# One level of Strassen's algorithm in the MLP of a hybrid decoder layer

## The chip, the cores and the metric

The kernel runs on one core of a Trainium2 chip. The metric is the device time of one execution in microseconds; the time of a kernel is the median of several runs. The profile is of one execution, and its span reaches from the first to the last instruction. The engines are called PE (matrix products; PEld is its loading of stationary operands), DVE, ACT, POOL and SP (which issues DMAs).

## The reference

One layer of a decoder trunk on 2048 prompt tokens and 64 sample tokens, model width 1024, in float32. A token mixer (dilated attention, an SSD scan, a short convolution, behind one input and one output projection) is followed by the MLP, which is what is changed:

```python
D_MODEL = 1024
D_FF = 4 * D_MODEL
...
        x = x + rms_norm(mix, norm_mix_post[l])
        h = rms_norm(x, norm_mlp_pre[l])
        f = jnp.square(jax.nn.relu(h @ w_mlp_up[l])) @ w_mlp_down[l]
        x = x + rms_norm(f, norm_mlp_post[l])
```

Further outputs are the attention caches shifted by eight tokens (16 copies of 2 MB from DRAM to DRAM) and the new states.

## The kernel before, in words

Every large product of float32 matrices is made of three matrix products of split operands: `A.copy` rounds an operand to its high part (type float32r), and a subtraction gives the low part. `mm3` (line 241) then issues hi x lo, hi x hi and lo x hi into one PSUM bank, the first argument being the stationary operand.

There are three stages. The *front* (`front`, line 1205) is the input projection with convolutions, SSD and prompt attention, in four blocks of 512 tokens. Then comes the *output projection* with the sample's attention, tile by tile of 128 tokens; it writes the rows `x2_d` to DRAM. Then the *MLP*. Work is written by generators: a main one emits a little tensor work per step, side streams are advanced in between (`stream`, `poll`). A stream yields how many microseconds of tensor work, by a formula of the kernel's own (columns / 2400, times 4 for plain float32, transposes columns / 1200), shall pass before its next step. Tile's scheduler then fixes the order of instructions on each engine and in each queue from its own estimate of time, and places the semaphores. All of a tag's tiles share that tag's slots; a new tile waits until a slot's last reader is done.

The MLP before goes over four blocks of tokens (512, 512, 512, 576; `MBlk`, line 1467) and in each over 16 groups of 256 of the 4096 hidden columns. `mlp_up` (line 1557) loads and splits, for 128 hidden columns at a time, the up weights (1024 x 128) and the down weights (128 x 1024), each as two raw tiles of 128 x 512 (`split_w`, line 1509: ACT casts, POOL subtracts); it accumulates over eight contraction chunks, and squares the ReLU. In the last block the columns go as 2 x 288. `mlp_down` (line 1581) runs one group behind: for each tile of 128 tokens and each half of the 1024 output columns it multiplies the group's two hidden chunks and adds the bank to an accumulator in SBUF. `mlp_out` (line 1599) norms a finished tile and adds the residual. Tokens are transposed on the tensor engine (`turn`, line 283). `mlp_ahead` (line 1529) prepares the first tokens and weights of the MLP while the output projection still runs.

## Time and profile before

| | |
|---|---|
| time, median of 3 runs | 2829.78 us (2826.06 to 2832.83) |
| span of the profiled execution | 2816.5 us; the profile gives no other time of that execution |
| PE busy | 2691.1 us, 96% of the span, 14369 matmuls |
| DVE, ACT, POOL busy | 51%, 37%, 45% |
| granted PE clock, mean | 0.983 |
| DMA | 419.16 MB, all of it issued by SP |
| first matmul of the MLP | 1285.3 us |

A row of a group reads: line, engine, operation, output <- inputs, shape, count, then busy time and the mean duration of one in ns, then the engine's idle time just before and what ended it. A row of a timeline begins with its start and its length in us. In the views by window the first two columns are the window and its length, then busy time and count of each engine, the granted PE clock, the share of the DMA engines' time and GB/s. Tile views give minimum, median and maximum duration in ns. Line numbers are those of the kernel before.

### The profile page before, as it was taken

What the parts mean: (1) busy time and instruction counts of PE and PEld (TensorE: products, weight loads), DVE (VectorE), ACT (ScalarE), POOL (GpSimd) and SP (SyncE); (2) the same over time, 40 slices, a digit from 0 to 9 for tenths busy, and PEclk for the clock granted to TensorE, in tenths of its full rate; (3) what the DMA queues carried; (4) which work ended last, traced back from release to release, by engine and by line L of the source; (5) the groups of instructions that cost most, each with busy time, mean ns of one, the idle gap of its engine ahead of it and who ended that gap; (6) DMA issues with size and microseconds to landing.
All of it is one profiled execution on the core that took longest, in us unless ns stands there. A gap on an engine that the chain in (4) does not pass through costs nothing.

```text
span 2816.5 us, 39903 instructions
## 1 busy us (share of the span) xinstructions
PE 2691.1 (96%) x14369; PEld 2218.0 (79%) x14369; DVE 1429.8 (51%) x2675; ACT 1049.0 (37%) x2386; POOL 1262.1 (45%) x1218
## 2 busy tenths in 40 slices
PE   7998999999999879999999999999999999999997
PEld 6997777778878646567888887888878888888886
DVE  4645445456554665554443463444554345554555
ACT  3534335345454223344233343322523334232232
POOL 4545443333554432236444464444654446343443
PEclk9999999999999989999999999999999999999998
DMA  6646975555555286455334454333443445332331
GB/s 189 178 134 210 265 208 163 150 182 180 159 180 148 93 247 202 143 188 184 127 90 130 132 170 126 124 127 120 153 142 120 132 130 166 108 113 69 119 112 42
DMA packets 445744, 419.16 MB, mean 149 GB/s; under 512 B 64427, under 2 KB 370131, under 8 KB 445033
## 3 DMA queue, kind: packets, MB, share of 16 engines
q1 hardware_dynamic: 445544, 416.61, 48.2%
q8 instruction: 113, 1.85, 0.3%
q14 instruction: 87, 0.70, 0.1%
HBM read 347.50 MB, written 102.43 MB: 160 GB/s over the span
## 4 chain that ended last, share of the span: by engine, by line
PE 57%; DMA 12%; issue 10%; POOL 9%; DVE 8%; ACT 3%; SPq 1%; POOLq 0%; ACTq 0%; DVEq 0%
PE pu L111 19%; PE pd L111 19%; PE po L111 6%; PE pj L111 6%; DMA raw<-in_w_mlp_up 3%; DMA wraw<-in_w_in 3%; PE pk L111 3%; POOL d L1523 2%; POOL u L1523 2%; PE pt L115 2%; POOL wlo L363 2%; DMA m<-o_d 1%; DVE xh L578 1%; POOL acc L1613 1%; DVE bc L804 1%
## 5 line engine op out<-in xcount | busy, mean ns | idle before, releaser
L111 PE MATMUL pu<-h2i,u 128*128 128x512 f32 (+1 forms) x2560 | 702.1, 356 | 2.2 <-POOL u L1523 2.2
L111 PE MATMUL pd<-d,fhi 128*128 128x512 f32 (+1 forms) x2176 | 676.8, 392 | 0.1
L1523 POOL TENSOR_TENSOR d<-raw,d 128x512 fp32r<-128x512 f32 x256 | 330.4, 1321 | 576.0 <-ACT d L1522 576.0
L1595 DVE TENSOR_TENSOR acc<-acc,pd 128x512 f32<-128x512 f32 (+1 forms) x510 | 347.1, 684 | 375.9 <-PE pd L111 375.0
L111 PEld LDWEIGHTS pu<-h2i,u 128*128 128x128 f32 x2560 | 455.8, 188 | 76.4 <-POOL u L1523 3.9
L111 PEld LDWEIGHTS pd<-d,fhi 128*128 128x128 f32 (+1 forms) x2176 | 397.8, 185 | 89.3 <-DVE acc L1593 1.4
L111 PE MATMUL pu<-h2l,u 128*128 128x512 f32 (+1 forms) x1280 | 456.8, 357 | 6.9 <-ACT u L1522 3.3
L111 PE MATMUL pd<-d,flo 128*128 128x512 f32 (+1 forms) x1088 | 425.5, 392 | 0.0
L1523 POOL TENSOR_TENSOR u<-raw,u 128x512 fp32r<-128x512 f32 x256 | 333.0, 1313 | 178.6 <-ACT u L1522 177.5
L363 POOL TENSOR_TENSOR wlo<-wraw,whi 128x512 fp32r<-128x512 f32 (+1 forms) x191 | 258.7, 1366 | 306.7 <-ACT whi L362 255.7
L1576 DVE TENSOR_TENSOR rl<-rl 128x512 f32<-128x512 f32 (+1 forms) x160 | 187.2, 1171 | 356.3 <-ACT fhi L1575 355.4
L1522 ACT CAST d<-raw 128x512 fp32r<-128x512 f32 x256 | 141.2, 617 | 562.8 <-issue 331.7
L1522 ACT CAST u<-raw 128x512 fp32r<-128x512 f32 x256 | 158.6, 620 | 344.2 <-DMA raw<-in_w_mlp_up 342.6
L111 PEld LDWEIGHTS pu<-h2l,u 128*128 128x128 f32 x1280 | 241.0, 188 | 46.4 <-ACT u L1522 4.1
L111 PE MATMUL pj<-lo,whi 128*128 128x512 f32 (+1 forms) x720 | 269.6, 374 | 6.1 <-ACT xr L572 4.5
L111 PE MATMUL pj<-hi,wlo 128*128 128x512 f32 (+1 forms) x720 | 259.8, 361 | 0.0
L111 PE MATMUL pj<-hi,whi 128*128 128x512 f32 (+1 forms) x720 | 259.4, 360 | 0.0
L111 PEld LDWEIGHTS pd<-d,flo 128*128 128x128 f32 (+1 forms) x1088 | 201.2, 185 | 47.4
L362 ACT CAST whi<-wraw 128x512 fp32r<-128x512 f32 (+1 forms) x192 | 114.4, 617 | 155.8 <-DMA wraw<-in_w_in 124.4
L111 PEld LDWEIGHTS pj<-lo,whi 128*128 128x128 f32 x720 | 137.3, 191 | 26.6 <-ACT xr L572 6.7
L111 PEld LDWEIGHTS pj<-hi,wlo 128*128 128x128 f32 x720 | 137.3, 191 | 18.3 <-issue 0.7
L111 PEld LDWEIGHTS pj<-hi,whi 128*128 128x128 f32 x720 | 137.5, 191 | 15.4
(298 smaller groups left out, 3986.4 us busy)
## 6 DMA issues: line engine op xcount, KB each, us to landing
raw<-in_w_mlp_up SPq DMA_DIRECT2D x256, 256.0 KB
raw<-in_w_mlp_down SPq DMA_DIRECT2D x256, 256.0 KB
wraw<-in_w_in SPq DMA_DIRECT2D x192, 256.0 KB
out_s_k<-in_cache_attn_k SPq DMA_DIRECT2D x8, 2040.0 KB
out_s_v<-in_cache_attn_v SPq DMA_DIRECT2D x8, 2040.0 KB
xt<-in_x_prompt SPq DMA_DIRECT2D x16, 512.0 KB
xc_d<-th SPq DMA_DIRECT2D x32, 256.0 KB
bc<-acsT_d SPq DMA_DIRECT2D x16, 512.0 KB
```

The lines of the kernel that those rows point to most:

```text
L111: return self.eng.matmul(out, lhsT, rhs, **kw)
L115: return self.eng.transpose(out, in_, identity)
L362: A.copy(hi[:, ks, :], raw)
L363: (V if not loaded and j else G).tensor_sub(lo[:, ks, :], raw, hi[:, ks, :].bitcast(F32))
L578: V.scalar_tensor_tensor(xh[:, :512], xr[:, j:j + 512], cwh(j, c), xh[:, :512], op0=ALU.mult, op1=ALU.add)
L804: V.tensor_scalar(bc[:, h, :], bc[:, h, :], acs[:, i, h:h + 1], 0.0, op0=ALU.subtract, op1=ALU.min)
L1522: A.copy(hi[:, cs], raw)
L1523: G.tensor_sub(lo[:, cs], raw, hi[:, cs].bitcast(F32))
L1576: V.tensor_mul(rl[:, :n], rl[:, :n], rl[:, :n])
L1595: V.tensor_add(B.accs[i][:n, cs], B.accs[i][:n, cs], ps[:n])
L1613: (V if hf and n == TS else G).tensor_add(acc[:n, cs], acc[:n, cs], xr[:n, cs])
```

## The change

The tokens are taken in three blocks of 704 (2 halves of 352, the last with the 64 sample tokens). Both products of the MLP are done as a 2 x 2 block product by Winograd's form of Strassen's algorithm: seven products of half-sized blocks instead of eight, with sums of blocks on both sides. For the up product the tokens are halved into 352 and 352, the contraction into 512 and 512, the hidden columns into 2048 and 2048; for the down product the contraction into 2048 and 2048 and the output into 512 and 512.

* The sums of weight blocks (four for each weight, 4 MB each) are formed in DRAM in the front, in a stream of its own: `weight_sums` copies a quarter of a block on SP's queue, then adds another block to it with an accumulating DMA on POOL's, and so on. The quarters 1, 2 and 3 are read straight from the weights.
* A block is a list of steps: for each of seven up products eight steps, then for each of seven down products eight. In step n the raw weights of step n+4 are loaded (one tile of 128 x 1024, 512 KB) and those of step n+1 split, by ACT and POOL (up) or ACT and DVE (down).
* An up step has two hidden chunks of 128 columns, each four contraction chunks of `mm3` with 352 moving columns; a down step has two contraction chunks for three token tiles (128, 128, 96), with 512 moving columns, and a product stays in its three PSUM banks over all its eight steps.
* Sums on the token side are formed by DVE in place (`up_sums`, `down_split`), sums of results by DVE from PSUM (`up_out`, `down_out`). A product's token operands are split by `s_pair`.
* Cache shifts are issued every 20 steps. Comments and docstrings are removed.

The diff, cut to its core (of the removed functions nothing is shown; they are in the code above):

```diff
+HT = 352
+BT = 2 * HT
+NSP = 12
...
+    wsum = {m: [dpool.tile(shape, F32, name=f"{m}{i}_d") for i in range(1, 5)]
+            for m, shape in (("u", [D // 2, FF // 2]), ("d", [FF // 2, D // 2]))}
...
+    def weight_sums():
+        for m in "ud":
+            n = wsum[m][0].shape[0] // 4
+            (b11, b12), (b21, b22) = corners[m]
+            w1, w2, w3, w4 = wsum[m]
+            for at in range(4):
+                r = slice(n * at, n * at + n)
+                nc.sync.dma_start(w1[r], b11[r])
+                nc.sync.dma_start(w3[r], b12[r])
+                yield 15.0
+                G.dma_start(w1[r], b12[r], accum_op=ALU.add)
+                G.dma_start(w3[r], b22[r], accum_op=ALU.add)
+                yield 20.0
+                nc.sync.dma_start(w2[r], w1[r])
+                yield 15.0
+                G.dma_start(w2[r], b22[r], accum_op=ALU.add)
+                yield 20.0
+                nc.sync.dma_start(w4[r], w2[r])
+                yield 15.0
+                G.dma_start(w4[r], b21[r], accum_op=ALU.add)
+                yield 15.0
+    corners = {}
+    for m, w in (("u", I["w_mlp_up"][0]), ("d", I["w_mlp_down"][0])):
+        r, c = w.shape
+        corners[m] = [[w[i * r // 2:(i + 1) * r // 2, j * c // 2:(j + 1) * c // 2] for j in range(2)]
+                      for i in range(2)]
+    quarters = {m: {1: corners[m][0][0], 2: corners[m][1][0], 3: corners[m][1][1],
+                    5: wsum[m][0], 6: wsum[m][1], 7: wsum[m][2], 4: wsum[m][3]} for m in "ud"}
...
         stream(side())
+        stream(weight_sums(), 40.0)
         yield from in_qkv(b0)
...
+    NJ = FF // P // 2
+    TP = [(0, P), (P, P), (2 * P, HT - 2 * P)]
+    UP_ORDER, DOWN_ORDER = (1, 2, 6, 7, 5, 3, 4), (1, 2, 7, 4, 5, 6, 3)
...
+    steps = [(kind, b, i, jj) for b in range(TT // BT) for kind, order in (("u", UP_ORDER), ("d", DOWN_ORDER))
+             for i in order for jj in range(NJ // 2)]
...
+    def w_load(at):
+        kind, b, i, jj = steps[at]
+        raw = w4.tile([P, 1024], F32, name="wraw4", tag="w")
+        if kind == "u":
+            wload[0] = nc.sync.dma_start(raw.rearrange("p (k c) -> p k c", c=2 * P),
+                                         quarters["u"][i].rearrange("(k p) c -> p k c", p=P)
+                                         [:, :, 2 * P * jj:2 * P * jj + 2 * P])
+        else:
+            wload[0] = nc.sync.dma_start(raw.rearrange("p (j c) -> p j c", c=512),
+                                         quarters["d"][i][2 * P * jj:2 * P * jj + 2 * P, :]
+                                         .rearrange("(j p) c -> p j c", p=P))
+        wts[at] = raw
+    def w_split(at):
+        raw = wts[at]
+        hi = w4.tile([P, 1024], F32R, name="whi4", tag="w")
+        lo = w4.tile([P, 1024], F32R, name="wlo4", tag="w")
+        A.copy(hi, raw)
+        (G if steps[at][0] == "u" else V).tensor_sub(lo, raw, hi.bitcast(F32))
+        wts[at] = hi, lo
+    def s_pair(src):
+        hi = s4.tile([P, HT], F32R, name="shi", tag="s")
+        lo = s4.tile([P, HT], F32R, name="slo", tag="s")
+        A.copy(hi, src)
+        V.tensor_sub(lo, src, hi.bitcast(F32))
+        return hi, lo
...
+            self.q = [], []
...
+                pt = ps.tile([P, 512], F32, name=f"pq{k}", tag=tag)
+                for xt, a, n in self.xs:
+                    PE.transpose(pt[:, a:a + n], xt[:n, k * P:(k + 1) * P], ident[:n, :n])
+                q = (r4 if self.t == 0 else f4).tile([P, HT], F32, name="q", tag="f")
+                A.activation(q, pt[:, :HT], AF.Copy, scale=vec[:, V_MLP + k:V_MLP + k + 1])
+                self.q[k // 4].append(q)
+                yield 1.0
...
+        s4 = p4.enter_context(sb("s4", NSP, "right"))
+        r4 = p4.enter_context(sb("r4", 8, "right"))
+        w4 = p4.enter_context(sb("w4", 8, "right"))
+        h = halves[0, 0] = Half(0, 0, [(w4, "w")])
+        h.rows()
+        yield 12.0
+        yield from h.turn(psS, "s")
+        up_s[0, 1] = [s_pair(q) for q in h.q[0]]
+        for at in range(4):
+            w_load(at)
+        w_split(0)
...
+    f4 = p4.enter_context(sb("f4", 64, "left"))
+    y4 = p4.enter_context(sb("y4", 12, "left"))
+    t4 = p4.enter_context(sb("t4", 2, "left"))
     psD = p4.enter_context(psb("ps4D", 4))
...
+    def bank():
+        nbank[0] += 1
+        ps, tag = ((psS, "s"), (psD, "pd"), (psD, "pd"))[nbank[0] % 3]
+        return ps.tile([P, 512], F32, name="pm", tag=tag)
...
+    def relu2(x, sign):
+        A.activation(x, x, AF.Relu, scale=sign)
+        A.activation(x, x, AF.Square)
+    def up_out(i, j, ps):
+        ps = ps[:, :HT]
+        x = {k[:2]: v for k, v in X.items() if k[2] == j}
+        if i == 1:
+            A.copy(f_tile(1, 2, j), ps)
+        elif i == 2:
+            o = f_tile(1, 1, j)
+            V.tensor_add(o, ps, x[1, 2])
+            relu2(o, 1.0)
+        elif i == 6:
+            V.tensor_add(x[1, 2], ps, x[1, 2])
+        elif i == 7:
+            V.tensor_add(f_tile(2, 1, j), ps, x[1, 2])
+        elif i == 5:
+            o = f_tile(2, 2, j)
+            V.tensor_sub(o, x[2, 1], ps)
+            V.tensor_sub(x[1, 2], x[1, 2], ps)
+            relu2(o, -1.0)
+        elif i == 3:
+            V.tensor_add(x[1, 2], ps, x[1, 2])
+            relu2(x[1, 2], -1.0)
+        else:
+            V.tensor_add(x[2, 1], ps, x[2, 1])
+            relu2(x[2, 1], 1.0)
+    def up_sums(b):
+        (q11, q12), (q21, q22) = halves[b, 0].q, halves[b, 1].q
+        s3 = []
+        for c in range(4):
+            s3.append(f4.tile([P, HT], F32, name="s3", tag="f"))
+            V.tensor_sub(s3[c], q11[c], q21[c])
+            V.tensor_sub(q21[c], q21[c], q22[c])
+            V.tensor_sub(q11[c], q21[c], q11[c])
+            V.scalar_tensor_tensor(q12[c], q12[c], -1.0, q11[c], op0=ALU.mult, op1=ALU.subtract)
+        return {6: q11, 7: s3, 5: q21, 3: q12, 4: q22}
+    def up_split(b, i, cs):
+        up_s.setdefault((b, i), []).extend(s_pair(src[b, i][c]) for c in cs)
...
+    def down_split(b, i, j):
+        x = {k[:2]: v for k, v in X.items() if k[2] == j}
+        if i == 1:
+            a = x[1, 1]
+        elif i == 2:
+            a = x[1, 2]
+        elif i == 7:
+            a = t4.tile([P, HT], F32, name="d3", tag="t")
+            V.tensor_sub(a, x[1, 1], x[2, 1])
+        elif i == 4:
+            a = x[2, 2]
+        elif i == 5:
+            a = x[2, 1]
+            V.tensor_sub(a, a, x[2, 2])
+        elif i == 6:
+            a = x[1, 1]
+            V.tensor_sub(a, x[2, 1], a)
+        else:
+            a = x[1, 2]
+            V.scalar_tensor_tensor(a, a, -1.0, x[1, 1], op0=ALU.mult, op1=ALU.subtract)
+        down_s[b, i, j] = s_pair(a)
+    def down_out(i, p, ps):
+        n = TP[p][1]
+        ps = ps[:n]
+        def y(t, d, new=False):
+            if new:
+                Y[t, d, p] = y4.tile([P, 512], F32, name=f"y{t}{d}", tag="y")
+            return Y[t, d, p][:n]
+        if i == 1:
+            A.copy(y(1, 2, True), ps)
+        elif i == 2:
+            V.tensor_add(y(1, 1, True), ps, y(1, 2))
+        elif i == 7:
+            V.tensor_add(y(2, 2, True), ps, y(1, 2))
+        elif i == 4:
+            V.tensor_add(y(2, 1, True), ps, y(2, 2))
+        elif i == 5:
+            for d in ((2, 2), (1, 2)):
+                V.tensor_sub(y(*d), y(*d), ps)
+        elif i == 6:
+            for d in ((2, 1), (2, 2), (1, 2)):
+                V.tensor_add(y(*d), ps, y(*d))
+        else:
+            V.tensor_add(y(1, 2), ps, y(1, 2))
...
+    for at, (kind, b, i, jj) in enumerate(steps):
+        if at + 4 < len(steps):
+            w_load(at + 4)
+        if at + 1 < len(steps):
+            w_split(at + 1)
+        order = UP_ORDER if kind == "u" else DOWN_ORDER
+        nxt = steps[at + 2] if at + 2 < len(steps) else None
+        if kind == "u" and jj == NJ // 2 - 2 and i != UP_ORDER[-1]:
+            ni = UP_ORDER[UP_ORDER.index(i) + 1]
+            if ni == 6:
+                while b not in done_in:
+                    advance(min(streams, key=lambda st: st[1]))
+                src.update({(b, k): v for k, v in up_sums(b).items()})
+            up_split(b, ni, (0, 1))
+        if kind == "d" and i == DOWN_ORDER[-1] and jj == NJ // 2 - 1 and (b + 1, 1) in src:
+            up_split(b + 1, 1, (0, 1))
+        two = steps[at + 1] if at + 1 < len(steps) else None
+        if kind == "u":
+            hi, lo = wts.pop(at)
+            s = up_s[b, i]
+            for j2 in range(2):
+                ps = bank()
+                for c in range(4):
+                    ws = slice(2 * P * c + P * j2, 2 * P * c + P * j2 + P)
+                    mm3(ps[:, :HT], hi[:, ws], lo[:, ws], *s[c], c == 0, c == 3)
+                up_out(i, 2 * jj + j2, ps)
+        else:
+            hi, lo = wts.pop(at)
+            if jj == 0:
+                banks = [bank() for _ in TP]
+            for j2 in range(2):
+                j = 2 * jj + j2
+                s = down_s.pop((b, i, j))
+                ws = slice(512 * j2, 512 * j2 + 512)
+                for p, (a, n) in enumerate(TP):
+                    mm3(banks[p][:n], s[0][:, a:a + n], s[1][:, a:a + n], hi[:, ws], lo[:, ws], j == 0, j == NJ - 1)
+            if jj == NJ // 2 - 1:
+                for p in range(len(TP)):
+                    down_out(i, p, banks[p])
+        if kind == "u" and jj == NJ // 2 - 1 and i != UP_ORDER[-1]:
+            up_split(b, UP_ORDER[UP_ORDER.index(i) + 1], (2, 3))
+        if kind == "d" and i == DOWN_ORDER[-1] and jj == NJ // 2 - 1 and b + 1 < TT // BT:
+            while (b + 1, 1) not in src:
+                advance(min(streams, key=lambda st: st[1]))
+            have = len(up_s.get((b + 1, 1), []))
+            up_split(b + 1, 1, range(have, 4))
+        if two is not None and two[0] == "d":
+            for j2 in range(2):
+                down_split(two[1], two[2], 2 * two[3] + j2)
+        if kind == "d" and jj == NJ // 2 - 1 and i in (6, 3):
+            for p in range(len(TP)):
+                mlp_out(b, 2 if i == 6 else 1, p)
+        if kind == "d" and i == 6 and jj == 2 and b + 1 < TT // BT:
+            stream(next_block(b + 1))
+        if at % 20 == 10 and shifts:
+            ...
```

More of the change, by code (lines that the diff above doesn't have):

```diff
@@ L1581, in mlp_down @@
-    def mlp_down(B, grp):
-        fs = B.f.pop(grp)
-        if B.accs is None:
-            B.accs = [accp.tile([P, D], F32, name=f"acc{i}", tag="acc") for i in range(len(B.tiles))]
-        for i, (t, n) in enumerate(B.tiles):
-            a = t - B.t0
-            for hf in range(2):
-                cs = slice(512 * hf, 512 * hf + 512)
-                ps = psD.tile([P, 512], F32, name="pd", tag="pd")
-                for c, (fhi, flo, dh, dl) in enumerate(fs):
-                    mm3(ps[:n], fhi[:, a:a + n], flo[:, a:a + n], dh[:, cs], dl[:, cs], c == 0, c == GC - 1)
-                if grp == 0:
-                    V.tensor_copy(B.accs[i][:n, cs], ps[:n])
-                else:
-                    V.tensor_add(B.accs[i][:n, cs], B.accs[i][:n, cs], ps[:n])
-            if grp == NG - 1:
-                mlp_out(B.accs[i], t, n)
@@ L1599, in mlp_out, with f_tile @@
-    def mlp_out(acc, t, n):
+    V.tensor_scalar(g4[:, 512:], g4[:, 512:], -1.0, None, op0=ALU.mult)
+    nbank = [0]
+    def bank():
+        nbank[0] += 1
+        ps, tag = ((psS, "s"), (psD, "pd"), (psD, "pd"))[nbank[0] % 3]
+        return ps.tile([P, 512], F32, name="pm", tag=tag)
+    XT = [(epool, "xres"), (epool, "x2t")]
+    X = {}
+    Y = {}
+    def f_tile(t, f, j):
+        X[t, f, j] = (r4 if (t, f) == (2, 2) and j >= 12 else f4).tile([P, HT], F32, name=f"x{t}{f}", tag="f")
+        return X[t, f, j]
@@ L1602, in mlp_out @@
         for hf in range(2):
[L1603 to L1604 removed]
+            A.activation(jk[:n, 512 * hf:512 * hf + 512], ys[hf][:n], AF.Square, accum_out=ss[:n, hf:hf + 1])
         G.tensor_add(ss[:n, 0:1], ss[:n, 0:1], ss[:n, 1:2])
         r = rstd_of(e4, ss[:, 0:1], n, D)
[L1607 to L1609 removed]
+        pool, tag = XT[xi[0] % 2]
@@ L1610, in mlp_out @@
+        xi[0] += 1
+        xr = pool.tile([P, D], F32, name="x2r", tag=tag)
+        nc.sync.dma_start(xr[:n], x2_d[t0:t0 + n, :])
         for hf in range(2):
             cs = slice(512 * hf, 512 * hf + 512)
-            V.scalar_tensor_tensor(acc[:n, cs], acc[:n, cs], r[:n], g4[:n, cs], op0=ALU.mult, op1=ALU.mult)
-            (V if hf and n == TS else G).tensor_add(acc[:n, cs], acc[:n, cs], xr[:n, cs])
-            nc.sync.dma_start(out[:, cs], acc[:n, cs])
-    B = early["B"]
-    prev = None
@@ new lines, in second_half, with next_block @@
+    def second_half(b):
+        h = halves[b, 1] = Half(b, 1, XT)
+        h.rows()
+        yield 10.0
+        yield from h.turn(psT, "tr")
+        done_in.add(b)
+    def next_block(b):
+        h = halves[b, 0] = Half(b, 0, XT)
+        h.rows()
+        yield 16.0
+        yield from h.turn(psT, "tr")
+        src[b, 1], src[b, 2] = h.q
+        yield from second_half(b)
+    done_in = set()
+    src[0, 2] = halves[0, 0].q[1]
+    stream(second_half(0))
+    for at, (kind, b, i, jj) in enumerate(steps):
[53 more added lines that the diff above has]
+        if at % 20 == 10 and shifts:
+            nm, sr, sb_ = shifts.pop(0)
+            with tc.issue_after(wload[0].ins):
+                nc.sync.dma_start(O[nm][0, sb_, 0:WB - NS].rearrange("t h e -> t (h e)"),
+                                  I[sr][0, sb_, NS:WB].rearrange("t h e -> t (h e)"))
+        poll()
@@ L1638, in hybrid_layer @@
+    drain()
+    assert not shifts
     p4.close()
```

151 lines of the change are left out of this document (31 added, 120 removed).

## The prediction

> **What bounds the kernel now.** I read the page's totals first, then busy time by stage, then the rhythm of single matmuls.
>
> ```profile
> span 2816.5 us, 39903 instructions
> PE 2691.1 (96%) x14369; PEld 2218.0 (79%) x14369; DVE 1429.8 (51%) x2675; ACT 1049.0 (37%) x2386; POOL 1262.1 (45%) x1218
> DMA  6646975555555286455334454333443445332331
> PE 57%; DMA 12%; issue 10%; POOL 9%; DVE 8%; ACT 3%; SPq 1%; POOLq 0%; ACTq 0%; DVEq 0%
> ```
>
> ```profile
> core 0: us, PE busy (x) PEld busy (x) DVE busy (x) ACT busy (x) POOL busy (x), PEclk, DMA share, GB/s
> 0.00:1000.00 1000.00, 916.38 (x5740) 788.41 (x5740) 541.18 (x1328) 444.75 (x1138) 442.27 (x486) 0.97 0.60 176
> 1000.00:1285.00 285.00, 267.25 (x1422) 177.54 (x1421) 156.18 (x401) 101.46 (x292) 77.18 (x109) 0.97 0.58 185
> 1285.00:2802.00 1517.00, 1507.50 (x7208) 1252.06 (x7208) 724.64 (x942) 501.44 (x953) 733.50 (x614) 1.00 0.39 125
> ```
>
> The stage from 1285 us on is the MLP. The tensor engine is busy there 1507.5 of 1517 us at granted clock 1.00, the DMA engines only 0.39 of the time: it is a tensor-engine stage, so fewer matmul columns are worth their full time as long as nothing else takes over. The stage before it, where the weight sums are put, is another matter: 84 of its first 1000 us pass with the tensor engine idle, and DMA is at 0.60, up to 0.9 in a slice of 70 us.
>
> The chain of waits names the same engine with only 57%, but it gives the rest to feeders that the engine never waits for; busy time by stage is the better guide here.
>
> A matmul's recorded duration overlaps its neighbour's, so I take the spacing of starts. These are the first and last rows of undisturbed stretches of the timeline:
>
> ```profile
> 1292.50 0.39 PE L111 MATMUL pu<-h2l,u 128*128 128x512 f32 x1
> ...
> 1302.30 0.39 PE L111 MATMUL pu<-h2l,u 128*128 128x512 f32 x1
> ...
> 2500.13 0.29 PE L111 MATMUL pu<-h2l,u 128*128 128x288 f32 x1
> ...
> 2503.30 0.30 PE L111 MATMUL pu<-h2l,u 128*128 128x288 f32 x1
> ...
> 2509.14 0.39 PE L111 MATMUL pd<-d,flo 128*128 128x512 f32 x1
> ...
> 2512.54 0.39 PE L111 MATMUL pd<-d,flo 128*128 128x512 f32 x1
> ```
>
> One such row comes in every three matmuls. Up, 512 columns: 42 matmuls in 9.80 us, 0.2333 us each. Up, 288 columns: 24 in 3.17 us, 0.132. Down, 512 columns: 15 in 3.40 us, 0.2267. The two up forms lie on a line (0.000452 us a column, 0.002 fixed), so 352 columns cost 0.161.
>
> ```profile
> L111 PE MATMUL pu<-h2i,u 128*128 128x512 f32 x1536 | 492.0, 396 | 2.2 <-POOL u L1523 2.2
> L111 PE MATMUL pu<-h2i,u 128*128 128x288 f32 x1024 | 210.2, 295 | 0.0
> L111 PE MATMUL pd<-d,fhi 128*128 128x512 f32 (+1 forms) x2176 | 676.8, 392 | 0.1
> L111 PEld LDWEIGHTS pu<-h2i,u 128*128 128x128 f32 x2560 | 455.8, 188 | 76.4 <-POOL u L1523 3.9
> L115 PE MATMUL pt<-cst,xt 128*128 128x128 f32 x256 | 45.7, 293 | 14.3 <-DVE xt L280 11.7 <-DVE lo L296 2.7
> ```
>
> **The change part by part: matmuls.** One of mm3's three products has rows of its own (h2l, flo) at half the count of the rows shown, so before there are 2304 up matmuls of 512 columns, 1536 of 288, and 3264 down matmuls: 2304 x 0.2333 + 1536 x 0.132 + 3264 x 0.2267 = 537.5 + 202.8 + 740.0 = 1480.3 us. After, up: 3 blocks x 7 products x 16 column chunks x 4 contraction chunks x 3 = 4032 of 352 columns, 4032 x 0.161 = 649. Down: 3 x 7 x 16 contraction chunks x 3 token tiles x 3 = 3024 of 512, 685.5. Together 1334.5: **-146 us**. Down gains less than an eighth (7.4%) because 352 tokens cut into 128, 128 and 96, and the 96 pay as much as 128. Transposes, 45.7/256 = 0.18 us each: 136 become 144, +1.4; in the MLP stage 104 become 120. The weight loads (188 ns recorded) don't set the rhythm: 288 columns already come every 132 ns.
>
> The rows before the MLP's end also give what it loses now: 1514.6 us from the first up matmul (1285.3) to the last down one (2799.9, below), less 1480.3, less 104 x 0.18 = 15.6 us.
>
> The Trainium skill ("TensorE: Matmul & The Clock Gate", section Back-to-back issue gap) gives a warm gap of N/2.4 + 2.5 ns; the rows here are longer (233 ns where it has 216). By its figures the saving would be an estimated 135 us, so the sum by it ends 11 us higher; I go by the rows.
>
> **Feeding an up step.** A step is 24 matmuls, 24 x 0.161 = 3.86 us. In it one 1024-wide raw tile is cast by ACT and subtracted by POOL. The output projection's weights show both at that width:
>
> ```profile
> L1069 ACT CAST wohi<-woraw x8: 1028/1042/1052, 931.6 to 968.3; 128x1024 fp32r<-128x1024 f32 x8
> L1070 DVE TENSOR_TENSOR wolo<-woraw,wohi x4: 1225/1432/2804, 933.3 to 965.4; 128x1024 fp32r<-128x1024 f32 x4
> L1070 POOL TENSOR_TENSOR wolo<-woraw,wohi x4: 2350/2384/2627, 934.5 to 969.4; 128x1024 fp32r<-128x1024 f32 x4
> ```
>
> The pool w4 has 8 slots: at any time four raw tiles, and hi and lo of the running step and of the next. So hi of step n+1 goes where hi of step n-1 was, and its cast can start when step n-1's last matmul ends. Then 1.04 + 2.4 + about 0.15 for two handovers = 3.6 us. It is first wanted 3.86 us (hi) and 3.86 + 0.32 (lo, the third matmul) later. Slack about 0.55 us, thin. ACT is in order: in steps of products 2, 5, 3 and 4 it also has two squared ReLUs of two operations each.
>
> ```profile
> L1574 ACT ACTIVATE rl<-pu 128x288 f32<-128x288 f32 x64 | 26.0, 408 | 33.3 <-PE pu L111 31.3 <-DVE flo L1577 2.1
> L1575 ACT ACTIVATE fhi<-rl 128x288 fp32r<-128x288 f32 x64 | 28.4, 445 | 1.9
> L1595 DVE TENSOR_TENSOR acc<-acc,pd 128x512 f32<-128x512 f32 x480 | 326.9, 685 | 349.2 <-PE pd L111 348.4
> ```
>
> At 352 columns about 0.47 each, so ACT has 1.04 + 4 x 0.47 = 2.9 of 3.86 us. The cast is free to start as the step turns, the last output's ReLU only about 0.6 us later (a PSUM add first), so I take the cast as first in line: nothing on the path, but 0.1 us a step for slips, 168 x 0.1 = 17 us. If the order were the other, see the second rival.
>
> DVE's own subtractions share SBUF with POOL. The same 288-wide form beside a POOL subtraction, and alone:
>
> ```profile
> 2498.78 2.76 POOL L1523 TENSOR_TENSOR d<-raw,d 128x512 fp32r<-128x512 f32 x2
> 2498.84 1.53 DVE L1576 TENSOR_TENSOR rl<-rl 128x288 f32<-128x288 f32 x1 [1.95 <-ACT fhi L1575]
> ...
> 2505.21 0.46 DVE L1576 TENSOR_TENSOR rl<-rl 128x288 f32<-128x288 f32 x1
> ```
>
> POOL subtracts 2.4 of each 3.86 us in up steps, so such an operation of 352 columns lies between 0.55 and 0.55 x 1.53/0.46 = 1.8 us, near 1.2 in the mean. On the path these are: the second half of the operand pairs at 18 changes of product, which may only start in the last step (0.5 us each, 9 us); and up_sums, sixteen such operations, ten of them with the first pairs ahead of the next product, 12 us against the 7.7 us of the two steps in which they are emitted: 5 us a block, 15 us. Additions that read PSUM keep 0.68 us whatever POOL does.
>
> The Trainium skill ("SBUF — State Buffer", section Terms) calls the DVE and POOL port pair an exclusive lock, held for the full instruction. By that a subtraction beside a 1024-wide one would wait up to its whole length, not half of a pair as above; by an estimate these two terms would then grow from 24 to about 40 us. This is the page that speaks most against the change, and the rows bear it out in kind.
>
> **Feeding a down step.** 18 x 0.2267 = 4.08 us. ACT 1.04 + 2 x 0.47; DVE one 1.23 us subtraction and two to four of 0.55, POOL idle: hidden. Where a product ends it isn't: product 6 brings 9 additions of 0.685 = 6.2 us to DVE, ahead of the next weights' low part (1.23) and the pairs; about 3 us late, product 5 (6 of them) 1 us, the rest 0.5: 13 us over three blocks. Changes of block, 1.5 us x 3 = 4. All stalls: 17 + 9 + 15 + 13 + 4 = 58 us where there are 15.6 now: **+42**.
>
> **Weight loads.** 512 loads of 256 KB (134 MB) become 336 of 512 KB (176 MB), 131-136 GB/s at full pace beside 125 now at a share of 0.39; rows of the up tiles grow from 512 to 1024 bytes. Issued four steps ahead, some 12 us. The 16 cache shifts stay, a load queued behind one on SP waits for it:
>
> ```profile
> 1320.00:1330.00 10.00, 10.00 (x45) 7.94 (x44) 3.52 (x6) 2.69 (x5) 5.04 (x4) 1.00 0.97 326
> 1340.00:1350.00 10.00, 10.00 (x45) 8.11 (x44) 3.48 (x6) 3.85 (x8) 6.08 (x5) 1.00 0.28 81
> ```
>
> One shift (2.09 MB) fills the DMA engines for under 10 us, less than the lead. Price nothing, covered by that lead; without it, some 3 us x 16.
>
> **The weight sums in the front.** 32 copies of 1 MB on SP's queue and 32 accumulating ones on POOL's, 67 MB of payload. Their emission is paced by estimated matmul time: 40 + 8 x 100, against about 890 of the whole front (my addition of its matmuls with the kernel's own formula), so all goes in ahead of the output projection. The shift above is the nearest row for a copy: 2.09 MB for (0.97 - 0.28) x 10 = 6.9 us of all engines, so 33.5 MB take 110 us. An accumulating one is not in the trace; it reads its target too, so between one and four copies' time, 110 to 440 us. The front has 1000 x 0.40 = 400 us free: sum 220 to 550. So from both sides: hidden (0; a gain is excluded, since nothing leaves the front), or 150 us over. I take it near the lower end, twice a copy, 330 of 400, since it is spread evenly. It still delays others:
>
> ```profile
> ACT whi L362 <- DMA wraw<-in_w_in: 124.4, 71, 6.2
> SPq L358 <- POOL wlo L363: 135.1, 89, 6.7
> PE pk L111 <- DVE dtall L516: 16.6, 5, 6.8
> ```
>
> The input weights arrive just in time: ACT waits for them 71 times. Behind a pair of copies on SP a load is up to 7 us later; POOL's queue holds the wlo subtractions behind each accumulating issue, and that waits for its copy; SP in turn stands at the copy into the next sum until the accumulation has landed. There are 24 such bursts. With three weight pieces in hand (each 24 x 0.2333 = 5.6 us of matmuls) most is absorbed; I put 1 us a burst on the path: **+25** (0 to 90).
>
> **Start and end.** The MLP's first tokens and weights are prepared within the output projection as now, from rows of the first three tiles: no change. The tail:
>
> ```profile
> 2799.54 0.40 PE L111 MATMUL pd<-d,flo 128*64 128x512 f32 x1
> ...
> 2812.67 1.15 SPq L1614 DMA_DIRECT2D out_y_sample<-acc  x2
> ```
>
> 13 us from the last matmul to the last store. After, three token tiles end together instead of one: **+3**.
>
> **Sum.** -146 + 1.4 + 42 + 25 + 3 = -74. The span of 2816.5 becomes 2742. The runs' median of 2829.8 is 13.3 us above the span, and what lies around it stays: 2756.
>
> **The rivals.** *All hidden.* Stalls as now (15.6) and a free front: -146 + 1.4 + 3 = -142, 2688. For it: an engine that is 99% fed now, and DMA at 0.39 in the MLP. Against it: 0.55 us of slack.
>
> *The weight split becomes the bound of the up steps (the other side).* If ACT does the last output's ReLUs (0.6 + 2 x 0.47 = 1.5 us) before the cast, lo is ready 1.5 + 0.1 + 3.5 = 5.1 us after the turn, 0.9 after the third matmul wants it. In all 168 steps +151 - 17: 2756 + 134 = 2890. In the 96 steps with ReLUs alone +69: 2825. It decides from (74 + 17)/168 = 0.54 us a step. For it: a chain of 3.6 in 3.86 us, through two in-order engines. Against it: the cast is ready first.
>
> *The front becomes a DMA stage.* Accumulation at three to four copies' time: 605 + 110 + 385 = 1100 us of DMA in 1000, +85 once pauses count, in place of 25: 2816. For it: the slice at 0.9 and the waits above; against it: the even spread.
>
> *The change doesn't do what it says:* 352-column matmuls paced by the weight load, 188 ns: +110, 2866. Excluded, nearly, by the 132 ns rhythm.
>
> **How the numbers follow.** My forecast 0.50 (by itself 2720 to 2800); all hidden 0.17; split-bound 0.16, of which 0.05 only in part and still faster or level; front 0.13, mostly still faster by half a percent; weight load 0.02; 0.02 beyond. Faster by over 0.2% (5.7 us, about what a measurement of this kernel tells from nothing): 0.50 + 0.17 + 0.03 + 0.09 = 0.79. Within: 0.04. Slower: 0.17. Range 2690 to 2845: it leaves out the full split-bound case and the lowest corner.
>
> **What would show it.** Right: rows of 352 columns every 0.161 us; the MLP's tensor engine above 95% busy; POOL's 1024-wide subtraction near 2.4 us ending before the third matmul of its step; idle gaps of 1 to 5 us at ends of products; the front 20 to 30 us longer. Wrong: PE waiting on lo of the weights in most up steps; DVE subtractions at 2.5 us and more; SP or POOL standing for accumulating DMAs, with the out projection starting 80 us late.

## The result, and the profile after

The changed kernel is slower: 3001.9 us (median, 2998.6 to 3005.4) beside 2829.2 us (2826.1 to 2832.8) for the kernel before in the same session, a ratio of 1.061 (95% interval 1.060 to 1.063). The prediction was 2756 us, range 2690 to 2845: a gain was forecast and a loss came, outside the range.

From the page of the changed kernel: its span, its busy totals (engine, busy us, share of the span, instructions), and three rows of its 40 slices of 75 us each.

```profile
span 2996.8 us, 40429 instructions
PE 2583.9 (86%) x14329; PEld 2189.5 (73%) x14329; DVE 1537.5 (51%) x3001; ACT 1317.8 (44%) x2741; POOL 1049.4 (35%) x908
PE   3013698998999999799999999988999999999997
PEclk7556899999999999899999999999999999999999
DMA  9999746875565654565544444455444446454443
```

The tensor engine is busy 107 us less than before (2583.9 for 2691.1), and the span is 180 us longer. The slices say where: the first five have PE at 0 to 6 tenths, and DMA at 9 in the first four.

Next, busy time by stage of the changed kernel (columns as in the prediction's second fence), first by its three stages (front, output projection, MLP), then the front again in three parts:

```profile
0.00:1205.00 1205.00, 899.37 (x5599) 778.39 (x5600) 512.99 (x1264) 430.26 (x1094) 451.99 (x495) 0.88 0.72 196
1205.00:1533.00 328.00, 297.78 (x1568) 199.45 (x1567) 173.69 (x439) 112.48 (x315) 92.48 (x129) 0.97 0.58 183
1533.00:2984.00 1451.00, 1386.75 (x7165) 1211.70 (x7164) 842.50 (x1292) 774.22 (x1332) 497.18 (x276) 0.99 0.48 159
...
0.00:200.00 200.00, 43.21 (x230) 36.75 (x230) 21.99 (x48) 23.82 (x47) 40.62 (x52) 0.64 1.01 261
200.00:400.00 200.00, 101.44 (x671) 95.83 (x672) 56.92 (x145) 50.78 (x130) 54.30 (x68) 0.73 0.85 211
400.00:1205.00 805.00, 754.72 (x4700) 645.81 (x4700) 434.07 (x1072) 355.65 (x917) 357.07 (x376) 0.97 0.61 176
```

I mark the stages by one group of matmuls, the output projection's (first and last start, from the view of the tile `wohi`; the row of before, then that of after):

```profile
L111 PE MATMUL po<-wohi,clo x272: 387/399/775, 956.9 to 1282.6; 128*128 128x512 f32 x128, 128*64 128x512 f32 x8
```

```profile
L115 PE MATMUL po<-wohi,clo x272: 386/398/629, 1207.0 to 1532.6; 128*128 128x512 f32 x128, 128*64 128x512 f32 x8
```

| | before | after | difference | predicted |
|---|---|---|---|---|
| front, to the first of these | 956.9 | 1207.0 | +250 | +25 |
| output projection | 325.7 | 325.6 | 0 | 0 |
| MLP, from the last of these to the last matmul (2799.5; 2981.4) | 1516.9 | 1448.8 | -68 | about -103 |
| from there to the span's end | 17.0 | 15.4 | -2 | +3 |

The front is the case. All the sums' DMAs run in its first 320 us, although they are emitted over nearly the whole of it. (In this part line numbers are those of the run's own kernel.) The view of the copies of L1220 and of the last accumulations L1232 (forms of the instruction; min, median and max of its ns; first and last start in us):

```profile
L1220 SPq DMA_DIRECT2D u_d<-in_w_mlp_up x4: 573/604/3691, 15.4 to 23.6; - x4
L1220 SPq DMA_DIRECT2D d_d<-in_w_mlp_down x4: 652/2484/33656, 26.4 to 127.2; - x4
...
L1232 POOL DMA_DIRECT2D d_d<-in_w_mlp_down x4: 1012/1012/1014, 275.4 to 304.9; - x4
```

A copy from weights in DRAM into DRAM depends on nothing, so the scheduler, which orders each engine's instructions itself, sets it as early as the queue lets it. The generator's pauses bind the order of emission only. SP then stands at one issue for up to 33.7 us, with the input weights' loads behind it. POOL stands 170 us in all, waiting before its 32 accumulations until earlier DMAs have landed, with its low-part subtractions behind it. The waits in the first 400 us (us in total, times, longest) are those of late loads and of what follows from them:

```profile
ACT whi L369 <- DMA wraw<-in_w_in: 134.3, 25, 38.6
PE pv L119 <- DMA pr<-in_state_ssm_conv: 70.2, 1, 70.2
PE pk L115 <- DVE dtall L523: 64.7, 2, 46.1
PE pk L115 <- POOL wlo L370: 60.6, 4, 29.9
```

Before, ACT waited 6.2 us at the longest for such a weight tile; now 38.6. The granted clock is down to 0.64 and 0.73 in these stretches, so the matmuls that do run cost more as well.

The MLP, waits of the tensor engine from 1533 us on:

```profile
PE pm L115 <- DVE wlo L1528: 24.5, 9, 6.4
PE pm L115 <- POOL wlo L1528: 15.3, 13, 2.5
PE pm L115 <- DVE slo L1536: 11.0, 5, 4.7
PE pq L119 <- DVE xt L287: 6.1, 3, 3.9
PE pm L115 <- ACT whi L1527: 3.6, 6, 0.9
PE pm L115 <- DVE x2t L1157: 1.3, 1, 1.3
```

Together 61.8 us. I went through all starts of the MLP: those that come over a tenth later than usual (0.161 us at 352 columns, 0.232 at 512) are late by 90 us in sum. So 28 more pass in matmuls that follow each other slowly, with hardly a wait; 14 of them lie in the eight stretches of 3.4 or 6.8 us in which the granted clock was 0.50. The timeline behind the wait for `xt` shows a part of these:

```profile
1604.95 0.58 PE L119 MATMUL pq<-cst,xt 96*128 96x96 f32 x2 [3.89 <-DVE xt L287]
...
1606.27 0.50 PE L115 MATMUL pm<-shi,wlo 128*128 128x352 f32 x1
1606.56 0.49 PE L115 MATMUL pm<-slo,whi 128*128 128x352 f32 x1
...
1608.49 0.32 PE L115 MATMUL pm<-shi,whi 128*128 128x352 f32 x1
1608.65 0.32 PE L115 MATMUL pm<-shi,wlo 128*128 128x352 f32 x1
```

and by windows around it:

```profile
1604.00:1609.00 5.00, 4.04 (x18) 4.05 (x19) 5.00 (x11) 2.76 (x7) 0.35 (x1) 0.66 0.35 105
1609.00:1614.00 5.00, 4.97 (x31) 4.68 (x31) 4.59 (x11) 4.30 (x9) 3.01 (x1) 1.00 0.00 2
```

After 3.89 us of idling, 352 columns come every 0.29 us for about 3 us, then every 0.16; the granted clock of these 5 us is 0.66, then 1.00. The Trainium skill ("TensorE: Matmul & The Clock Gate", section What's actually happening) puts the engine at half its clock after an idle window of some 3.4 us, until it has been busy for as long; 352 columns at the half clock that it states would be an estimated 0.293 us, and the trace agrees.

### The profile page after: what moved, and what is told of

Its sections match the earlier page's. It is cut to its first block, busy times and chain, and to the rows that moved or that the text cites. A ratio compares the mean times of both kernels' runs of the same rounds, so it can differ in the third digit from the quotient of the medians.

```text
span 2996.8 us, 40429 instructions
## 1 busy us (share of the span) xinstructions
PE 2583.9 (86%) x14329; PEld 2189.5 (73%) x14329; DVE 1537.5 (51%) x3001; ACT 1317.8 (44%) x2741; POOL 1049.4 (35%) x908
## 3 DMA queue, kind: packets, MB, share of 16 engines
q0 software_dynamic: 10752, 33.56, 6.0%
## 4 chain that ended last, share of the span: by engine, by line
PE 46%; DVE 7%; DMA 4%; POOL 3%; ACT 2%; issue 2%; SPq 0%; POOLq 0%; ACTq 0%; DVEq 0%
PE pm L115 39%; PE po L115 4%; DMA m<-o_d 1%; DVE wlo L1528 1%; POOL wlo L1528 1%; DMA xt<-x_d 1%; DVE slo L1536 1%; POOL rstd L259 1%; POOL rstd_ms L258 0%; PE psq L115 0%; DMA kn<-in_cache_attn_k 0%; PE pt L119 0%; DVE x L1679 0%; ACT whi L1527 0%; PE pos L115 0%
## 5 line engine op out<-in xcount | busy, mean ns | idle before, releaser
L1527 ACT CAST whi<-wraw 128x1024 fp32r<-128x1024 f32 x336 | 351.9, 1047 | 349.3 <-PE pm L115 305.0
L1528 POOL TENSOR_TENSOR wlo<-wraw,whi 128x1024 fp32r<-128x1024 f32 x168 | 410.2, 2442 | 270.9 <-ACT whi L1527 239.7
L115 PE MATMUL pm<-slo,whi 128*128 128x352 f32 x1344 | 439.3, 327 | 14.3 <-DVE slo L1536 9.4
L115 PE MATMUL pm<-shi,whi 128*128 128x352 f32 x1344 | 437.3, 326 | 0.0
L115 PE MATMUL pm<-shi,wlo 128*128 128x352 f32 x1344 | 412.9, 328 | 15.4 <-POOL wlo L1528 15.3
L115 PE MATMUL pm<-wlo,shi 128*128 128x512 f32 (+1 forms) x1008 | 401.2, 398 | 24.6 <-DVE wlo L1528 24.5
L115 PE MATMUL pm<-whi,shi 128*128 128x512 f32 (+1 forms) x1008 | 399.9, 397 | 0.0
L115 PE MATMUL pm<-whi,slo 128*128 128x512 f32 (+1 forms) x1008 | 389.8, 397 | 1.7 <-DVE slo L1536 1.7
L115 PEld LDWEIGHTS pm<-slo,whi 128*128 128x128 f32 x1344 | 256.4, 191 | 17.1 <-DVE slo L1536 9.9
L115 PEld LDWEIGHTS pm<-shi,whi 128*128 128x128 f32 x1344 | 255.9, 190 | 0.1
```

Of the source, the lines that this page charges most:

```text
L115: return self.eng.matmul(out, lhsT, rhs, **kw)
L1527: A.copy(hi, raw)
L1528: (G if steps[at][0] == "u" else V).tensor_sub(lo, raw, hi.bitcast(F32))
```

## The experiments

Theory after the result: (a) the sums' DMAs, drawn forward and in volume, cost the front some 250 us; (b) Strassen's products themselves are worth their predicted gain in the MLP, less stalls at the changes of product. Rivals: the front's loss has another source in the change; the pace is innocent and the volume alone does it, or the reverse; the stalls come from DVE's many operations, as the prediction had it.

**No sums.** The stream of sums is left out, and the four sum quarters are replaced by plain blocks of the same shape.

```
-        stream(weight_sums(), 40.0)
-                    5: wsum[m][0], 6: wsum[m][1], 7: wsum[m][2], 4: wsum[m][3]} for m in "ud"}
+                    5: corners[m][0][1], 6: corners[m][0][0], 7: corners[m][1][0], 4: corners[m][1][1]} for m in "ud"}
```

> The changed kernel without the weight sums: no summing DMA is issued, and the four products that need sums read plain blocks of the weights instead, so the loads keep their number and size but the result of the MLP is another. Theory (the sums, drawn together into the first 305 us, cost the front 250 us): the output projection's first matmul falls from 1205 back to about 955 us, and the time from 3002 to about 2750. Rival (the new MLP is what is slow): the time stays near 3000.

Measured 2767.2 us, ratio 0.978 (0.977 to 0.980). The first output projection matmul (here and below that of the group `po<-wohi,chi`: 955.1 us before, 1205.4 changed) is back at 965.1 us. So the sums cost 235 us (3001.9 - 2767.2). Without them the kernel is 59 us faster than the kernel before in the same session (2826.6), and stands 36 us above the forecast without its term for the sums (2756 - 25 = 2731).

**The sums alone**, added to the kernel before (nothing reads them).

```
 (before)  stream(side())
+        stream(weight_sums(), 40.0)
```

> The kernel before with the weight-sum stream alone added, in the same place and without any tie; nothing reads the sums. Theory: the front is 250 us longer, time about 3080, and the summing DMAs stand at 15 to 305 us as in the changed kernel. Rival (the sums hurt only together with the new MLP's loads): 2830 to 2870.

Measured 3068.6 us (two runs), ratio 1.085 (1.083 to 1.087): 242 us more than before in the same session, the output projection starting at 1198.7 us. The sums' DMAs are issued between 14 and 300 us, as in the changed kernel. The loss in the front needs nothing else of the change.

**Paced.** Each copy is tied behind the last input weight load emitted before it on SP, each accumulation behind the last low-part subtraction of POOL.

```
-                nc.sync.dma_start(w1[r], b11[r])
+                with tc.issue_after(last["sp"].ins):
+                    nc.sync.dma_start(w1[r], b11[r])
...
-                G.dma_start(w1[r], b12[r], accum_op=ALU.add)
+                with tc.issue_after(last["pool"].ins):
+                    G.dma_start(w1[r], b12[r], accum_op=ALU.add)
```

> The changed kernel, but each copy of the sums is tied behind the last input-weight load that was emitted before it on SP, each accumulation behind the last weight subtraction on POOL, so the 64 transfers go in all along the front in place of its first 305 us. Same transfers, same bytes. Theory (their place is what costs): front 955 to 1010 us, time 2755 to 2810, faster than the kernel before. Rival (67 MB more are too much for the front, wherever they are put): front still above 1100, time 2950 or more.

Measured 2882.6 us, ratio 1.019 (1.017 to 1.021): 119 us of the 235 go, 115 stay. The first 200 us now look like this (by windows):

```profile
0.00:200.00 200.00, 171.26 (x1178) 159.48 (x1179) 93.00 (x223) 84.55 (x205) 85.29 (x100) 0.94 0.70 194
```

PE 171 us for 43, DMA 0.70 for 1.01. But the output projection starts at 1087.2 us, 122 later than without sums. Theory and rival are half right each, and the time lies between their ranges: the crowding at the front's start and the volume cost about the same. Whether the crowding costs by full DMA engines or by SP and POOL standing, no run separates.

**Paced, low parts of the down weights on POOL** (which has little to do in down steps; a try at relieving DVE).

```
-        (G if steps[at][0] == "u" else V).tensor_sub(lo, raw, hi.bitcast(F32))
+        G.tensor_sub(lo, raw, hi.bitcast(F32))
```

> As the paced kernel, and the down weights' low part is subtracted by POOL in place of DVE. Theory (the stalls of 4 to 6.6 us behind product 6 of each block, and smaller ones, come from DVE, which has nine additions of PSUM and then the subtraction): these stalls go, 15 to 30 us less than the paced kernel. Rival (POOL's 2.44 us and its hold on SBUF make new waits in 4.08 us steps, DVE's own subtractions first): the same or slower by up to 40 us.

Measured 2942.4 us, ratio 1.040 (1.038 to 1.042), 60 us more than paced: the rival's way, and beyond its 40 us. The tensor engine's longest group of waits in the MLP:

```profile
PE pm L115 <- POOL wlo L1539: 81.8, 28, 9.7
```

Where paced, the waits for both engines' `wlo` summed to 36.7 us. POOL takes 2.4 us for what DVE does in 1.2, and it also holds `mlp_out`'s residual additions in front of it. That pointed to these additions; it doesn't show them to be the cause.

**The residual additions on DVE**, on the kernel without sums.

```
-            (V if hf and b == TT // BT - 1 else G).tensor_add(o[:n], o[:n], xr[:n, cs])
+            V.tensor_add(o[:n], o[:n], xr[:n, cs])
```

> The kernel without weight sums (2767 us; MLP output differs: four sums replaced by plain blocks), with the last residual additions (y plus x2r) all on DVE instead of POOL. Theory: the 6.5 us stall behind product 6 and those of 4 us behind product 3 come from DVE's 1024-wide subtraction (1.21 us alone, 6.47 beside four POOL additions) losing SBUF to POOL. Then that subtraction takes about 1.2 us everywhere in down steps, the stalls shrink to 3 us or less, and the time is 2740 to 2757. Rival (the nine PSUM additions and DVE's queue are the cause, as the prediction had it): DVE gets six more operations at that place, the stall stays or grows, 2767 to 2785.

Measured 2738.9 us, ratio 0.969 (0.967 to 0.972), 28 us less than with the additions on POOL (25 by the ratios), 1 us below the theory's range. In the profiled executions 23 of the 28 lie in the MLP (1456.9 to 1433.9 us). In the kernel without sums, behind product 6 (from the timelines of DVE, POOL and PE):

```profile
1748.10 1.21 DVE L1527 TENSOR_TENSOR wlo<-wraw,whi 128x1024 fp32r<-128x1024 f32 x1
...
1753.71 6.47 DVE L1527 TENSOR_TENSOR wlo<-wraw,whi 128x1024 fp32r<-128x1024 f32 x1
...
1754.17 4.92 POOL L1731 TENSOR_TENSOR y<-y,x2r 128x512 f32<-128x512 f32 x4
...
1760.23 0.79 PE L115 MATMUL pm<-wlo,shi 128*128 128x512 f32 x1 [6.41 <-DVE wlo L1527]
```

and at the same place with the additions on DVE:

```profile
1752.11 1.22 DVE L1527 TENSOR_TENSOR wlo<-wraw,whi 128x1024 fp32r<-128x1024 f32 x1
...
1753.38 0.50 PE L115 MATMUL pm<-wlo,shi 128*128 128x512 f32 x1 [1.27 <-DVE wlo L1527]
```

One subtraction took 6.47 us beside four back-to-back additions of POOL, and takes 1.22 without them. DVE got six operations more there, and the tensor engine's wait of 6.41 us shrank to 1.27 us; the rival falls. POOL's additions end at 1759.09, and 1.21 us later DVE's would end if it had waited for all four: 1760.30, where it ended at 1760.18. The Trainium skill ("SBUF — State Buffer", section Terms) says that the loser of the shared port pair fully blocks; this row agrees, and DVE was kept out over four instructions of POOL.

**Token tiles written out one a step, operand sums three steps sooner**, on top of that.

```
-                mlp_out(b, 2 if i == 6 else 1, p)
+            later = [(b, 2 if i == 6 else 1, p) for p in range(len(TP))]
+        elif later:
+            mlp_out(*later.pop(0))
...
+        if kind == "u" and i == 2 and jj == NJ // 2 - 5:
+            ... src.update({(b, k): v for k, v in up_sums(b).items()})
```

> The same, and two moves in emission: the finished token tiles are written out one a step instead of three at the product's end, and the operand sums of an up phase are made three steps sooner. Theory (stalls are late work of DVE at the change of a product): the 4.8 us wait behind the operand sums goes in two blocks, and the waits behind products 6 and 3 are below 1.5 us; 10 to 20 us below the run with the additions on DVE alone, 2725 to 2742. Rival (the operand sums share SBUF with POOL's weight subtractions wherever they stand, and only move their delay): within 5 us of that run.

Measured 2738.4 us, ratio 0.968 (0.965 to 0.971): no difference that can be measured. The waits of the tensor engine for `slo` in the MLP, of the run with the additions on DVE and of this one:

```profile
PE pm L115 <- DVE slo L1535: 11.1, 5, 4.7
```

```profile
PE pm L115 <- DVE slo L1535: 1.7, 3, 0.6
```

The waits of 4.7 us behind the operand sums did go, and the profiled MLP is 6.9 us shorter, but the front of that execution ran 4 us longer. By its number the rival holds, by its mechanism the theory; it stays undecided.

**Accumulating DMAs as plain copies**, on the paced kernel: the four `accum_op=ALU.add` are left out.

> The paced kernel (2883 us) with its 32 accumulating DMAs as plain copies on the same queue (the sums are wrong by that, the MLP output differs): same bytes written, no read of the target. Theory (the front's remaining 115 us is DMA time): the accumulating DMAs took 180 us of 16 engines and as copies take about 110, so 40 to 70 us come off: 2813 to 2843. Rival (order of issue and the chains between copies cost it, not time in the engines): within 15 us of 2883.

Measured 2823.1 us, ratio 0.999 (0.998 to 1.000), 60 us less (56 by the ratios), within the theory's range. POOL's queue in the paced kernel and here (packets, MB, share of 16 engines' span):

```profile
q0 software_dynamic: 10752, 33.56, 6.4%
```

```profile
q0 software_dynamic: 6656, 33.56, 3.4%
```

6.4% of 2879.8 is 184 us, 3.4% of 2824.1 is 96 us: accumulating costs 1.9 times a copy. 88 us less of DMA time made the kernel 60 us faster, 0.7 of it, where the sums as a whole cost 0.4 of theirs (115 of the 287 us below); why the accumulations weigh more is open. The copies on the other queues cost 103 us more in the paced kernel than in the one without sums (54.5% of 2879.8 less 53.0% of 2766.5), by these rows of the two pages:

```profile
q1 hardware_dynamic: 413896, 492.10, 54.5%
```

```profile
q1 hardware_dynamic: 408008, 458.54, 53.0%
```

Together the sums take 287 us of DMA time, where the prediction put 330.

**Placed.** Additions on DVE and the two moves, full sums. The sums run over four row pieces in turn, so that a dependent DMA is four places behind; those for the up weights go in the front, tied as in the paced kernel; those for the down weights go one every two steps into block 0's up phase.

```
+    def weight_sums(m):
+        for dst, src, add in ((w3, b12, b22), (w1, b11, b12), (w2, w1, b22), (w4, w2, b21)):
+            for at in range(4): ... nc.sync.dma_start(dst[r], src[r]); yield 24.0
+            for at in range(4): ... G.dma_start(dst[r], add[r], accum_op=ALU.add); yield 24.0
...
+        if at % 2 == 0:
+            last["sp"] = wload[0]
+            next(dsums, None)
```

> The whole change with full sums, placed otherwise: additions on DVE and the two moves as in the last run; the sums for the up weights paced over the front, each DMA tied behind the last weight load (SP) or low-part subtraction (POOL) emitted before it, four row pieces in turn so that a dependent DMA is four places behind; the sums for the down weights one DMA every two steps of block 0's up phase, where DMA was 0.4 to 0.56 busy. Theory: the cost of the sums is DMA time in excess of what a stage has free; half of the front's 115 us or less remains (20 to 57), the down sums cost 0 to 20 in the MLP: 2765 to 2815, below the kernel before. Rival: the down sums delay the MLP's weight loads, which are issued 12 us ahead, by bursts of 1 MB (up to 25 us landing): 32 delays of 2 to 5 us, 2830 to 2900.

Measured 2804.0 us, ratio 0.992 (0.989 to 0.994): 0.8% faster than before, clear of noise, and within the theory's range. The output projection starts at 1022.3 us, 56 later than the same kernel without sums (966.0); the MLP takes 1437 us for 1427. Some weight loads in the MLP were held up: with the DMA share at 1.00 from 1420 to 1520 us, the waits for the cast of the weights (`whi`) are 12.8 us in place of 7.0, the longest 6.4. That is far from 32 delays of 2 to 5 us, so the rival falls.

**The front's DMAs made small.** As placed, but each of the up sums' 32 DMAs carries a sixteenth of its rows, and the up products read plain blocks.

```
+                r = slice(n * at, n * at + (n if m == "d" else n // 16))
```

> As the placed kernel (2804 us, first output projection matmul at 1022 us), but each of the 32 DMAs of the up sums carries a sixteenth of its rows, and the up products read plain blocks (so the MLP's output differs). Places, ties, queues and chains of the DMAs stay. Theory (the front pays for DMA time): the output projection starts at 962 to 975 us, the time is 2742 to 2757. Rival (the front pays for the instructions in SP's and POOL's queues and for what stands behind their waits, whatever they carry): the start stays at 1005 us or later, the time above 2785.

Measured 2750.1 us, ratio 0.970 (0.966 to 0.975). The output projection starts at 963.1 us: with the places, ties, queues and chains as they were, the cost is gone. Once paced, the front pays for what the DMAs carry and not for the issues. Shorter DMAs also end waits in the queues sooner, but there was little to end: in the placed kernel POOL waited 0.8 us in all for a copy of the up sums.

**The up sums in the output projection**, one DMA every 8 us of matmuls, tied behind the token tiles' DMAs and additions.

```
-        stream(weight_sums("u"), 40.0)
 (output projection)
+        gap[0] = 8.0
+        stream(weight_sums("u"))
```

> As the placed kernel (2804 us), with the sums for the up weights moved out of the front into the output projection, one DMA about every 8 us of matmuls, tied behind the token tiles' loads, stores and additions. Theory: a sum costs where weight loads arrive just in time (front: 145 us of DMA time cost 58 us there) and little where only the DMA engines' total counts; the output projection has 0.44 of 327 us free, 145 us. So the front returns to about 962 us, the output projection grows by 5 to 30 us: 2750 to 2780. Rival (145 us of sums cost the same 58 us wherever weights or tokens are read meanwhile): 2795 to 2815.

Measured 2797.8 us, ratio 0.989 (0.987 to 0.991). The front is back at 964.5 us as the theory had it, but the output projection takes 367.5 us for 329.8. A window and a group of waits of it:

```profile
1000.00:1100.00 100.00, 70.08 (x307) 45.46 (x308) 45.67 (x128) 23.88 (x71) 28.20 (x40) 0.78 0.94 291
```

```profile
PE pkk L119 <- DMA kn<-in_cache_attn_k: 32.6, 4, 14.6
```

DMA is at 0.94 there, and the sample's cached keys come late. The MLP takes 12 us more than in the placed kernel as well; 9 of them are waits for its token rows (`xt`, 11.1 us for 1.9), 7.2 us in one of them right at its start. The total is the rival's, the split is neither's. Half of the sums, some 144 us of DMA time, cost 56 us in the front (0.39 of itself), 38 in the output projection (0.26) and 10 in block 0's up phase (0.07), where weights are issued four steps ahead; in two other runs with the down sums there the MLP is 9 (half and half) and 16 us (small DMAs) longer than the 1427.

**Half and half**: two of the four up sums in the front from 400 us of matmuls on, the others in the output projection.

```
+        usums.append(weight_sums("u"))
+        stream(itertools.islice(usums[0], 16), 400.0)
```

> As the placed kernel, with the first two of the four up sums in the front, from 400 us of matmuls on (DMA share 0.5 to 0.6 there), and the other two in the output projection at one DMA per 16 us. Theory (cost grows faster than the DMA share): the halves cost 10 to 25 us in the front and 0 to 10 in the output projection: 2752 to 2780. Rival (cost in proportion to the sums' DMA time, 0.4 of it in the front): front 29 and output projection 0, or 29 too: 2775 to 2804.

Measured 2785.2 us (2776.4 to 2793.0), ratio 0.983 (0.981 to 0.986). The front takes 32 us more, the output projection 15, each above the theory's share. The total is in the rival's range, and the front's part (0.44 of 72 us of DMA time) fits its proportional cost; it is still the fastest complete version, 1.7% below the kernel before and 217 us below the changed one.

## Why the prediction was wrong, by its own steps

The steps from the changed kernel to the best one without sums add up, in medians of runs. They come from several sessions, in which the kernel before differs by up to 5 us (2826.2 to 2831.1).

| step | us | change |
|---|---|---|
| the changed kernel | 3001.9 | |
| sums tied to their places | 2882.6 | -119 |
| accumulating DMAs as copies | 2823.1 | -60 |
| no sums | 2767.2 | -56 |
| residual additions on DVE | 2738.9 | -28 |

**The front: the step that failed.** The prediction took the emission to be "paced by estimated matmul time" and "spread evenly", and from that chose twice a copy's time, "330 of 400" us free, and 1 us a burst: +25, in a range of 0 to 90. Two things in it were false.
- Emission order was read as execution order. The sums ran between 15 and 320 us, and that cost 119 us over the same DMAs tied to their places. The prediction's own sign for it, "SP or POOL standing for accumulating DMAs, with the out projection starting 80 us late", came true in kind, with POOL standing 170 us before them and the output projection 250 us late; but the rival had the cause in the accumulation's price, and "against it: the even spread" kept it at 0.13. The upper bound of 150 us was the DMA time in excess of the whole front's; it wasn't the case of all of it coming at once, and the result of 250 lay above it.
- Free DMA time was taken as nearly free of cost. Evenly spread, the sums still cost 115 us for 287 us of DMA time. The prediction had them hidden as long as they fit into the free time, but for 1 us a burst. The small-DMA run shows that what is paid for is what the DMAs carry, not the bursts' instructions.

**The price of the volume: right.** Twice a copy was 1.9 times; 110 us for 33.5 MB of copies was 96 to 103.

**Matmuls, -146: close, about -137.** 352 columns come every 0.161 us, as taken. A down matmul of 512 columns was taken at 0.2267 us; in the changed kernel 45 of them take 10.46 us, 0.232 each:

```profile
1776.52 0.39 PE L115 MATMUL pm<-wlo,shi 128*128 128x512 f32 x1
...
1786.98 0.39 PE L115 MATMUL pm<-wlo,shi 128*128 128x512 f32 x1
```

Over 3024 matmuls that is 16 us more than put. By the mean spacing without the late starts, the MLP's matmuls take 1487 us before and 1350 after. Why 512 columns take 0.232 us here and 0.227 (median of the down matmuls) before is open. The transposes cost less than the 0.18 us put for each: 120 of them some 10 us, not 22. The two errors nearly cancel, so the MLP's total doesn't show them. (The 131 GB/s of a down step is 128, 512 KB in 4.08 us; nothing hangs on it.)

**The stalls of the MLP, 58 us: mis-sized, 90 measured.** The chain of cast and subtraction is no bound: in 168 steps of up, waits for POOL's `wlo` and for `whi` sum to 18.9 us, where 17 were put; the rival of 2890 us didn't occur. DVE's own subtractions, 24 put, cost 11.0 us of waits for `slo`; the operand sums' 5 us a block were 4.7 in two of the three blocks. Token rows cost 7.4 us, where 4 were put for changes of block. The ends of products cost 24.5 us of waits for DVE's `wlo`, where 13 were put. The term of product 6, "9 additions of 0.685 = 6.2 us to DVE", "about 3 us late", was 6.4 in two blocks, and its mechanism was another: POOL's residual additions holding up DVE's subtraction. In the prediction POOL counted as idle in down steps; `mlp_out` was not in that count. Moving them gave 28 us. And no term stood for the other 28 us, of which 14 passed at the lowered clock.

With -137 for the matmuls and stalls of 90 us in place of some 17, the MLP comes out some 66 us shorter; measured are 68.

**Start and end, +3:** -2, nothing.

With the front at its own +25, the changed kernel would have come out at 2767 + 25 = 2792 us: faster than before and inside the range, but 36 us above the forecast, by the MLP's part, which gained 68 us and not 103.

## What to carry to other kernels

A transfer that depends on nothing goes where the scheduler puts it, not where a generator emits it: before pricing background DMAs as spread out, find what ties each to its place, or give it a tie. Even spread out, DMA time in a stage with DMA engines partly free is not free; here it cost 0.3 to 0.4 of itself in the front, whose weights arrive just in time, 0.2 to 0.3 in the output projection, and 0.06 to 0.11 in the MLP's first up phase, whose loads run four steps ahead. That the lead makes the difference is argued, not shown: no run varied it. So an algorithm that saves a tenth of a stage's matmuls must be charged for the traffic that prepares it. At each stall look at what the other of DVE and POOL is doing in that very microsecond, epilogue work included.

## What the runs showed of the hardware

- An accumulating DMA from DRAM into DRAM: 33.56 MB took 184 us of 16 engines, a plain copy of the same bytes on the same queue 96 us.
- DVE's 128x1024 subtraction took 1.21 us alone and 6.47 us beside four additions of POOL.
- A matmul of 512 columns came every 0.232 us in the down products of the changed kernel and every 0.227 in those of the kernel before; why is open.
- One idle time of 3.9 us was followed by some 3 us at 0.29 us for 352 columns in place of 0.16, at a granted clock of 0.66.
